# A head of bias moved from GpSimd and VectorE to TensorE in a log-sum-exp kernel, and larger loads

## The chip, the cores and the metric

The kernel runs on one core of one Trainium2 chip. The metric is the device time of one execution in microseconds; the runs shown are summed up by their median.

## The reference

Every row of `x` (8 batches, 2048 rows, 2048 columns, float32) is cut into 8 heads of 256 columns. A bias row of 256 is added to each head, and the log of the sum of exponentials is taken over each head's 256 columns; every result stands twice in a row, since the heads are repeated along the rows.

```python
x_heads = x.reshape(B, S, H, Dh).transpose(0, 2, 1, 3)
x_heads = x_heads + bias[None, :, None, :]
x_tiled = np.repeat(x_heads, 2, axis=2)
mx = x_tiled.max(axis=-1, keepdims=True)
lse = mx.squeeze(-1) + np.log(np.exp(x_tiled - mx).sum(axis=-1))
```

## The kernel before

A tile is 128 partitions x 2 rows x 2048 columns, 2 MB; there are 64, 8 for each batch. Eight tile buffers lie in SBUF as four blocks `xb` of 4 MB. The exponential is taken without the maximum (a check at the end, `judge`, repeats all with it if any sum is out of range).

Each tile of the long stage, 0 to 53 (`BULK`), is shared out by heads:

- Heads 0 to 2: TensorE puts the bias into PSUM (`put_bias`, L370: `ones_bf` against `b3`, the bias as three bfloat16 rows; for tiles 0 and 1, before `b3` is there, three one-row matmuls from `bparts` instead) and adds x with an identity matmul (`late_heads`, L428, float32, two passes each). Head 0 is in the bank `one_ps`, heads 1 and 2 in one of two `pair` tiles. ScalarE takes head 0's exponential with its sum (L439, one for each of the 2 rows) and writes the exponentials of heads 1 and 2 back to the tile (L446).
- Head 3: ScalarE takes its exponential without the bias, in place, and VectorE multiplies by exp(bias), which lies in PSUM as `w_ps` (L496).
- Heads 4 to 7: GpSimd adds the bias in place (`g_add`, L478, `b_rep`), ScalarE takes the exponential (L484, one instruction with head 3).
- VectorE sums heads 1 to 7 in one reduction (L503).

The order of the instructions on each engine is the order in which the code writes them (`tc.manual_schedule`). For tile t it is: x matmuls of t, GpSimd's add of t, then `later` of tile t-1 (L484, L496, L503) with the issue of a load (`reload`), then ScalarE's part of t, then the bias matmuls of t+1. Loads are issued by SyncE (SP); tiles 2 to 41 come as 4 MB blocks (L228), issued once both tiles of the block's buffer are done, tiles 0, 1 and 42 to 56 as 2 MB (L243), later ones in smaller pieces. `BLOCKS` is that limit.

Tiles 54 to 56 (`MIXED`) have heads 0 and 1 on TensorE, heads 2 and 3 weighed by VectorE (`weigh`, L519) and heads 4 to 7 on GpSimd; tiles 57 to 60 go by single rows, and the tail, 61 to 63, has an order written by hand (`TAIL`). They need exp(bias) of other heads in PSUM: `first_factors` makes heads 1 and 2 in `one_ps` after tile 53 (spread by TensorE at L303, exponential at L335), `other_factors` the rest at tile 32.

At the start the bias row comes in one 8 KB transfer (`brow`, L280), GpSimd splits it into the three bfloat16 parts (L293 to L297), and TensorE spreads heads 4 to 7 over the partitions (`spread`, L303), from which VectorE copies `b_rep` (L309).

Of the kernel before, what the change touches and what calls it, by code (L numbers as in the profile page):

```python
# [9 lines left out]
F32 = mybir.dt.float32  # L10
BF16 = mybir.dt.bfloat16
I32 = mybir.dt.int32
ACT = mybir.ActivationFunctionType
# [3 lines left out]

K = 2
KB = 4
BLOCKS = 42  # L20

NBUF = 8

NEARLY = 2

WARM = 384

# [17 lines left out]
STAGES = [  # L45
    (0, (BULK,)),
    (54, (MIXED,)),
# [45 lines left out]
def kernel(  # L93
# [6 lines left out]
    nc = tc.nc  # L100
    P = nc.NUM_PARTITIONS
    B, S, D = x.shape
    H, Dh = bias.shape
# [18 lines left out]

    brow = sb.tile([1, D], F32, name="brow")
    b_rep = sb.tile([P, D - G0], F32, name="b_rep")
# [91 lines left out]

    loads = {}
# [3 lines left out]
    def load(t):  # L221
        if TB <= t < BLOCKS:

# [32 lines left out]
    def reload(t):  # L256

        n = t + NBUF
        if n < BLOCKS:
            if n % TB == TB - 1:  # L260
# [41 lines left out]
    def spread(dst, c0, c1):  # L302
        nc.tensor.matmul(  # L303
            dst, lhsT=ones, rhs=brow[:, c0:c1], start=True, stop=True
        )

    for i, c in enumerate(range(G0, D, MM)):
        spread(ps[i], c, c + MM)
        nc.vector.tensor_copy(b_rep[:, c - G0 : c - G0 + MM], ps[i])  # L309
    W_LATE = BULK["g0"] * Dh  # L310
    w_late = w_ps[:, 0 : W_LATE - W0]
    spread(w_late, W0, W_LATE)
    nc.scalar.activation(out=w_late, in_=w_late, func=ACT.Exp)

    nc.vector.memset(Rx[0][:, 0:1], 4.0)
    nc.vector.memset(Rx[0][:, 1 + widths[0] :], 4.0)
# [1 line left out]
        out=b_far,  # L318
        in_=brow,
# [5 lines left out]
        out=Rx[0][0:1, 1 + widths[0] :],  # L325
# [6 lines left out]

    def first_factors():
        spread(one_ps, V0, W0)
        nc.scalar.activation(out=one_ps, in_=one_ps, func=ACT.Exp)  # L335

    def other_factors():
        nc.scalar.activation(
            out=w_ps[:, W_LATE - W0 :], in_=b_rep[:, W_LATE - G0 : W2 - G0], func=ACT.Exp
        )  # L340
        nc.scalar.activation(out=w_sb, in_=b_rep[:, W1 - G0 :], func=ACT.Exp)

# [13 lines left out]
    def put_bias(m, k0, k1):  # L356

        if m["late"]:  # L360
            pair = pairs[n_ps[0] % 2]
            n_ps[0] += 1
            got = [one_ps, pair[:, 0:MM], pair[:, MM : 2 * MM]]

            parts = [(ones_bf, b3)]
            if n_ps[0] <= NEARLY:
                parts = [(ones_bf[0:1], bparts[:, i]) for i in range(3)]
            for h, p in enumerate(got):
                for i, (lhsT, b) in enumerate(parts):
                    nc.tensor.matmul(  # L370
                        p,
                        lhsT=lhsT,
                        rhs=each_row(b, h * Dh, Dh, K),
                        start=i == 0,
                        stop=False,
                    )
            return got + [pair]
        n = m["pe"] * Dh
        rows = min(k1 - k0, max(MM // n, 1))
        got = []  # L380
        for k in range(k0, k1, rows):
            for c in range(0, n, MM):
                w = min(n - c, MM)
                bank = n_ps[0] % len(ps)
                p = ps[bank][:, 0 : rows * w]
                n_ps[0] += 1
                mm = nc.tensor.matmul(
                    p,
                    lhsT=ones_bf,
                    rhs=each_row(b3, c, w, rows),  # L390
                    start=True,
                    stop=False,
                )
                on_bank(bank, mm)
                got.append((k, k + rows, c, w, bank, p))
        return got
# [26 lines left out]
    def late_heads(m, t, got, sums):  # L423


        mms = []
        for h, p in enumerate(got[:-1]):
            mm = nc.tensor.matmul(  # L428
                p,
                lhsT=ident,  # L430
                rhs=xts[t % NBUF][:, :, h * Dh : (h + 1) * Dh],
                start=False,
                stop=True,
            )
            mms.append(on_x(t, mm, [loads[t, 0, 0]]))

        def pe_part():
            for k in range(K):
                act = nc.scalar.activation(  # L439
                    out=xts[t % NBUF][:, k, 0:Dh],  # L440
                    in_=got[0][:, k * Dh : (k + 1) * Dh],
                    func=ACT.Exp,
                    accum_out=sums[:, k, 0:1],
                )
                last_uses[t].append(on_x(t, act, [mms[0]]))
            act = nc.scalar.activation(  # L446
                out=xts[t % NBUF][:, :, Dh : m["pe"] * Dh].rearrange(
                    "p k (h j) -> p h k j", j=Dh
                ),
                in_=got[-1].rearrange("p (h k j) -> p h k j", k=K, j=Dh),  # L450
                func=ACT.Exp,
            )
            on_x(t, act, [mms[-1]])

        return pe_part

# [10 lines left out]
    def each_row(src, c, n, k_rows):  # L467

        return bass.AP(
            tensor=src.tensor,  # L470
            offset=src.offset + c,
            ap=[src.ap[0], [0, k_rows], [1, n]],
        )

    def g_add(m, t, k0, k1):
        c = m["g0"] * Dh
        v = xts[t % NBUF][:, k0:k1, c:D]
        add = nc.gpsimd.tensor_tensor(  # L478
            out=v, in0=v, in1=each_row(b_rep, c - G0, D - c, k1 - k0), op=ALU.add
        )  # L480
        return on_x(t, add, [loads[t, k0, 0]])
# [3 lines left out]

    def later(m, t, k0, k1, sums, add):

        h0 = m["pe"] if m["late"] else m["g0"]
        v = xts[t % NBUF][:, k0:k1, h0 * Dh : D]
        done = exp_inplace(t, v, add)  # L490
        if m["late"]:
            n = (m["g0"] - h0) * Dh
            f = v[:, :, 0:n]
            h0 = m["acc"]
            v = xts[t % NBUF][:, k0:k1, h0 * Dh : D]
            mul = nc.vector.tensor_tensor(  # L496
                out=f,
                in0=f,
                in1=each_row(w_ps, m["pe"] * Dh - W0, n, k1 - k0),
                op=ALU.mult,  # L500
            )
            done = on_x(t, mul, [done])
        red = nc.vector.tensor_reduce(  # L503
            out=sums[:, k0:k1, h0:H],
            in_=v.rearrange("p k (h j) -> p k h j", j=Dh),
            op=ALU.add,
            axis=mybir.AxisListType.X,
        )
        last_uses[t].append(on_x(t, red, [done]))

    def weigh(t, v, h, dst, after):
        c = h * Dh
        if c < W0:
            w = one_ps[:, c - V0 : c - V0 + Dh]
        elif c < W2:
            w = w_ps[:, c - W0 : c - W0 + Dh]
        else:
            w = w_sb[:, c - W1 : c - W1 + Dh]
        ttr = nc.vector.tensor_tensor_reduce(  # L519
            out=v,  # L520
            in0=v,
            in1=w,
            scale=1.0,
            scalar=0.0,
            op0=ALU.mult,
            op1=ALU.add,
            accum_out=dst,
        )
        last_uses[t].append(on_x(t, ttr, [after]))
# [329 lines left out]
    for t in range(T_TAIL):  # L859
        if t == T_FACTORS:  # L860
            other_factors()
        xt = xts[t % NBUF]
        sums = sums_of(t)
        for k0, k1, c0, c1 in pieces(t):
            m = modes_of(t)[k0]
# [28 lines left out]
            h0 = m["pe"]  # L894
# [107 lines left out]
```

## Time and profile before

| | us |
|---|---|
| median of 3 runs (322.25 to 322.52) | 322.31 |
| profiled execution, its own time | 322.15 |
| its span | 320.3 |
| TensorE busy (matmuls) | 247.0 |
| VectorE busy | 286.3 |
| ScalarE busy | 264.1 |
| GpSimd busy | 287.4 |

The span is the stretch that the profile covers; the rest of the execution's time lies around it. Busy time is the sum over instructions that compute; matmuls overlap one another, so TensorE's is not its throughput. The core read 134.23 MB and wrote 1.05 MB. In the profile PE is TensorE (PEld its weight loads), DVE VectorE, ACT ScalarE, POOL GpSimd, SP SyncE; L478 is line 478 of the kernel before.

### The profile page before, as it was taken

Reading aid. Unit: us, or ns where it says so; the run is one execution under the profiler, and the core shown is the slowest. Engines: PE = TensorE matmul, PEld = TensorE weight load, DVE = VectorE, ACT = ScalarE, POOL = GpSimd, SP = SyncE. Lnnn points to the kernel's source line nnn. Section 1 sums busy time; section 2 is a strip of 40 time slices with the busy share of each in tenths; the row PEclk is TensorE's granted clock in tenths of the full one; section 3 lists DMA queues with packets and bytes.
Section 4 is the critical chain, followed back from the end, with each engine's and each line's share of the span. In section 5 each row is a group of like instructions: output and inputs, shape, how many; then the busy total and the mean of one; then the engine's idle time right before and its main releaser. Section 6 shows DMA issues by size and latency. Waiting matters only on the chain.

```text
span 320.3 us, 2291 instructions
## 1 busy us (share of the span) xinstructions
PE 247.0 (77%) x621; PEld 100.5 (31%) x622; DVE 286.3 (89%) x304; ACT 264.1 (82%) x437; POOL 287.4 (90%) x116
## 2 busy tenths in 40 slices
PE   5998884877886677868688776988777787688774
PEld 1333332323332223323233322443333332133332
DVE  1337999699989999998989999799999999999996
ACT  1159987798788888779879988699889898999996
POOL 7939997999999999999999989999999999986874
PEclk9979996899799999979979998799999999799999
DMA  7999999999999999999999999999999999999996
GB/s 302 440 438 458 397 455 436 413 454 405 450 450 401 455 411 438 454 409 443 446 410 450 413 440 450 403 430 428 434 436 432 425 430 429 425 429 427 424 415 229
DMA packets 8950, 135.44 MB, mean 423 GB/s; under 512 B 996, under 2 KB 1511, under 8 KB 2791
## 3 DMA queue, kind: packets, MB, share of 16 engines
q1 hardware_dynamic: 8784, 135.14, 98.7%
q10 hardware_dynamic: 152, 0.14, 0.1%
q8 instruction: 5, 0.08, 0.1%
q14 instruction: 9, 0.07, 0.1%
HBM read 134.23 MB, written 1.05 MB: 422 GB/s over the span
## 4 chain that ended last, share of the span: by engine, by line
DMA 42%; POOL 18%; ACT 18%; DVE 13%; PE 8%; issue 0%; SPq 0%
DMA xb<-in_x_dram 41%; POOL xb L478 18%; ACT xb L484 12%; DVE R L503 11%; ACT xb L459 4%; PE pair L428 3%; DVE xb L496 2%; PE one_ps L428 2%; PE pair L303 1%; PE pair L370 1%; ACT xb L446 1%; DMA brow<-in_bias_dram 1%; PE one_ps L370 1%; ACT xb L439 1%; PE w_ps L303 0%
## 5 line engine op out<-in xcount | busy, mean ns | idle before, releaser
L478 POOL TENSOR_TENSOR xb<-xb,b_rep 128x2048 f32<-128x2048 f32 x57 | 257.6, 4545 | 18.9 <-DMA xb<-in_x_dram 18.9
L503 DVE TENSOR_REDUCE R<-xb 128x14 f32<-128x3584 f32 (+1 forms) x57 | 216.8, 3804 | 1.9
L484 ACT ACTIVATE xb<-xb 128x2560 f32<-128x2560 f32 (+8 forms) x79 | 156.8, 1996 | 18.2 <-POOL xb L478 18.2
L428 PE MATMUL pair<-xb,ident 128*128 128x512 f32 x216 | 110.0, 635 | 0.0
L428 PE MATMUL one_ps<-xb,ident 128*128 128x512 f32 x108 | 62.4, 661 | 17.1 <-DMA xb<-in_x_dram 17.1
L446 ACT ACTIVATE xb<-pair 128x1024 f32<-128x1024 f32 x54 | 55.5, 1029 | 18.2 <-PE pair L428 18.2
L428 PEld LDWEIGHTS pair<-xb,ident 128*128 128x128 f32 x216 | 44.5, 206 | 58.2 <-issue 58.2
L496 DVE TENSOR_TENSOR xb<-xb,w_ps 128x512 f32<-128x512 f32 x54 | 36.7, 679 | 22.3 <-ACT xb L484 22.3
L370 PE MATMUL one_ps<-b,ones_bf 128*128 128x512 bf16 x52 | 19.9, 382 | 38.0 <-ACT xb L439 38.0
L439 ACT ACTIVATE xb<-one_ps 128x256 f32<-128x256 f32 x108 | 40.0, 378 | 7.1 <-PE one_ps L428 7.0
L370 PEld LDWEIGHTS <-ones_bf 128*128 128x128 bf16 (+1 forms) x174 | 17.5, 101 | 85.5 <-issue 78.4
L370 PE MATMUL pair<-b,ones_bf 128*128 128x512 bf16 x104 | 31.1, 381 | 0.0
L428 PEld LDWEIGHTS one_ps<-xb,ident 128*128 128x128 f32 x108 | 19.8, 200 | 31.8 <-DMA xb<-in_x_dram 25.5
L439 ACT ACTIVATION_READ_ACCUMULATOR xb<-one_ps 128x1 f32 x108 | 22.1, 204 | 0.0
L519 DVE CUSTOM_DVE_ANT_0 xb<-xb,w_ps 128x256 f32<-128x256 f32 x60 | 22.0, 415 | 0.0
L405 PE MATMUL pair<-xb,ident 128*128 128x512 f32 x28 | 16.3, 685 | 5.5 <-DMA xb<-in_x_dram 5.3
L542 POOL TENSOR_TENSOR xb<-xb 128x128 f32<-128x128 f32 (+3 forms) x36 | 14.1, 392 | 3.3 <-ACT xb L832 0.5
L459 ACT ACTIVATE xb<-pair 128x256 f32<-128x256 f32 x39 | 15.2, 412 | 0.0
L536 POOL TENSOR_TENSOR xb<-xb,w_sb 128x256 f32<-128x256 f32 (+1 forms) x11 | 9.1, 827 | 4.4 <-ACT xb L484 3.9
L821 PE MATMUL pair<-xb,ident 128*128 128x256 f32 (+1 forms) x22 | 8.0, 456 | 3.2 <-DMA xb<-in_x_dram 3.2
L419 PE MATMUL tp<-b_rep,ident 128*128 128x384 f32 x24 | 9.7, 485 | 0.0
L459 ACT ACTIVATION_READ_ACCUMULATOR xb<-pair 128x1 f32 x39 | 9.3, 240 | 0.0
(61 smaller groups left out, 81.5 us busy)
## 6 DMA issues: line engine op xcount, KB each, us to landing
xb<-in_x_dram SPq DMA_DIRECT2D x20, 4096.0 KB, 22.0
xb<-in_x_dram SPq DMA_DIRECT2D x17, 2048.0 KB, 21.4
xb<-in_x_dram SPq DMA_DIRECT2D x10, 1024.0 KB, 21.7
xb<-in_x_dram SPq DMA_DIRECT2D x2, 640.0 KB, 18.2
xb<-in_x_dram SPq DMA_DIRECT2D x3, 384.0 KB, 12.3
xb<-in_x_dram SPq DMA_DIRECT2D x1, 768.0 KB
xb<-in_x_dram SPq DMA_DIRECT2D x2, 256.0 KB, 15.5
out_dram<-res SPq DMA_DIRECT2D x1, 512.0 KB, 5.8
```

What stands on the lines that cost most here:

```text
L370: nc.tensor.matmul(p, lhsT=lhsT, rhs=each_row(b, h * Dh, Dh, K), start=i == 0, stop=False,)
L405: mm = nc.tensor.matmul(p, lhsT=ident, rhs=xts[t % NBUF][:, ka:kb, c : c + w], start=False, stop=True,)
L428: mm = nc.tensor.matmul(p, lhsT=ident, rhs=xts[t % NBUF][:, :, h * Dh : (h + 1) * Dh], start=False, stop=True,)
L439: act = nc.scalar.activation(out=xts[t % NBUF][:, k, 0:Dh], in_=got[0][:, k * Dh : (k + 1) * Dh], func=ACT.Exp, accum_out=sums[:, k, 0:1],)
L446: act = nc.scalar.activation(out=xts[t % NBUF][:, :, Dh : m["pe"] * Dh].rearrange("p k (h j) -> p h k j", j=Dh), in_=got[-1].rearrange("p ...
L459: act = nc.scalar.activation(out=xts[t % NBUF][:, k, h * Dh : (h + 1) * Dh], in_=p, func=ACT.Exp, accum_out=sums[:, k, h : h + 1],)
L478: add = nc.gpsimd.tensor_tensor(out=v, in0=v, in1=each_row(b_rep, c - G0, D - c, k1 - k0), op=ALU.add)
L484: return on_x(t, nc.scalar.activation(out=v, in_=v, func=ACT.Exp), [after])
L496: mul = nc.vector.tensor_tensor(out=f, in0=f, in1=each_row(w_ps, m["pe"] * Dh - W0, n, k1 - k0), op=ALU.mult,)
L503: red = nc.vector.tensor_reduce(out=sums[:, k0:k1, h0:H], in_=v.rearrange("p k (h j) -> p k h j", j=Dh), op=ALU.add, axis=mybir.AxisListTy ...
L519: ttr = nc.vector.tensor_tensor_reduce(out=v, in0=v, in1=w, scale=1.0, scalar=0.0, op0=ALU.mult, op1=ALU.add, accum_out=dst,)
L542: done = nc.gpsimd.tensor_tensor(out=v[:, :, 0:n], in0=v[:, :, 0:n], in1=v[:, :, n : 2 * n], op=ALU.add)
```

## The change

- Head 3 of the long stage goes to TensorE too: a fourth bias matmul and a fourth x matmul for each tile, into a bank of its own, `wa_ps`, and an exponential of its own on ScalarE. The bias goes into the banks in the order of heads 1, 2, 0, 3, and x in the order 0, 3, 1, 2. ScalarE's exponential in place shrinks from 5 to 4 heads.
- VectorE multiplies 128 columns of head 4 (`N_LATE`) by exp(bias) instead of the 256 of head 3, and GpSimd adds the bias to heads 4 to 7 without these 128 columns.
- PSUM: `w_ps` is split into the banks `wa_ps` and `wb_ps`. `wa_ps` is in use until tile 53, so the factors of heads 3 and 4 are made by a second spread and exponential in `first_factors`; those of head 5's first 128 columns by `last_factors` before tile 56.
- The bias row comes in two transfers of four heads each; `CPE`, the columns that GpSimd splits into bfloat16 parts and the width of `b3`, grows from 768 to 1024. The spread of head 3 at the start is dropped.
- `BLOCKS` is 48 instead of 42: tiles 42 to 47 come as 4 MB blocks.

```diff
-BLOCKS = 42
+BLOCKS = 48
...
+LATE_BIAS = (1, 2, 0, 3)
+LATE_X = (0, 3, 1, 2)
...
-BULK = dict(pe=3, acc=1, g0=4, late=True, fold=0)
+BULK = dict(pe=4, acc=1, g0=4, late=True, fold=0)
+N_LATE = 128
...
-    w_ps = pp.tile([P, W2 - W0], F32, name="w_ps")
+    wa_ps = pp.tile([P, MM], F32, name="wa_ps")
+    wb_ps = pp.tile([P, MM], F32, name="wb_ps")
+    WB = W0 + MM
...
-    nc.scalar.dma_start(
-        out=brow.rearrange("p (h j) -> p h j", h=H), in_=bias.unsqueeze(0)
-    )
+    for h in range(0, H, H // 2):
+        nc.scalar.dma_start(
+            out=brow.rearrange("p (h j) -> p h j", h=H)[:, h : h + H // 2],
+            in_=bias[h : h + H // 2].unsqueeze(0),
+        )
...
-    W_LATE = BULK["g0"] * Dh
-    w_late = w_ps[:, 0 : W_LATE - W0]
-    spread(w_late, W0, W_LATE)
-    nc.scalar.activation(out=w_late, in_=w_late, func=ACT.Exp)
+    w_late = wb_ps[:, 0:N_LATE]
+    nc.scalar.activation(out=w_late, in_=b_rep[:, 0:N_LATE], func=ACT.Exp)
...
     def first_factors():
         spread(one_ps, V0, W0)
+        spread(wa_ps, W0, WB)
         nc.scalar.activation(out=one_ps, in_=one_ps, func=ACT.Exp)
+        nc.scalar.activation(out=wa_ps, in_=wa_ps, func=ACT.Exp)
+
+    def last_factors():
+        nc.scalar.activation(
+            out=w_late, in_=b_rep[:, WB - G0 : WB - G0 + N_LATE], func=ACT.Exp
+        )
...
-            got = [one_ps, pair[:, 0:MM], pair[:, MM : 2 * MM]]
+            got = [one_ps, pair[:, 0:MM], pair[:, MM : 2 * MM], wa_ps]
...
-            for h, p in enumerate(got):
+            for h in LATE_BIAS:
+                p = got[h]
...
             act = nc.scalar.activation(
-                out=xts[t % NBUF][:, :, Dh : m["pe"] * Dh].rearrange(
+                out=xts[t % NBUF][:, :, 3 * Dh : 4 * Dh],
+                in_=got[3].rearrange("p (k j) -> p k j", j=Dh),
+                func=ACT.Exp,
+            )
+            on_x(t, act, [mms[3]])
+            act = nc.scalar.activation(
+                out=xts[t % NBUF][:, :, Dh : 3 * Dh].rearrange(
                     "p k (h j) -> p h k j", j=Dh
                 ),
...
-        c = m["g0"] * Dh
+        c = m["g0"] * Dh + (N_LATE if m["late"] else 0)
...
-                in1=each_row(w_ps, m["pe"] * Dh - W0, n, k1 - k0),
+                in1=each_row(wb_ps, 0, N_LATE, k1 - k0),
...
+        if t == T_ROWS - 1:
+            last_factors()
```

More of the change, by code (lines that the diff above doesn't have):

```diff
@@ L334, in first_factors @@
         spread(one_ps, V0, W0)
+        spread(wa_ps, W0, WB)
         nc.scalar.activation(out=one_ps, in_=one_ps, func=ACT.Exp)
+        nc.scalar.activation(out=wa_ps, in_=wa_ps, func=ACT.Exp)
[3 more added lines that the diff above has]
+        )
     def other_factors():
         nc.scalar.activation(
-            out=w_ps[:, W_LATE - W0 :], in_=b_rep[:, W_LATE - G0 : W2 - G0], func=ACT.Exp
+            out=wb_ps[:, N_LATE:], in_=b_rep[:, WB - G0 + N_LATE : W2 - G0], func=ACT.Exp
         )
@@ L423, in late_heads @@
     def late_heads(m, t, got, sums):
-        mms = []
-        for h, p in enumerate(got[:-1]):
+        mms = {}
+        for h in LATE_X:
             mm = nc.tensor.matmul(
-                p,
+                got[h],
                 lhsT=ident,
@@ L434, in late_heads @@
             )
-            mms.append(on_x(t, mm, [loads[t, 0, 0]]))
+            mms[h] = on_x(t, mm, [loads[t, 0, 0]])
         def pe_part():
@@ L452, in pe_part @@
             )
-            on_x(t, act, [mms[-1]])
+            on_x(t, act, [mms[2]])
         return pe_part
@@ L486, in later @@
     def later(m, t, k0, k1, sums, add):
-        h0 = m["pe"] if m["late"] else m["g0"]
+        h0 = m["g0"]
         v = xts[t % NBUF][:, k0:k1, h0 * Dh : D]
@@ L491, in later @@
         if m["late"]:
-            n = (m["g0"] - h0) * Dh
-            f = v[:, :, 0:n]
+            f = v[:, :, 0:N_LATE]
             h0 = m["acc"]
@@ L514, in weigh @@
             w = one_ps[:, c - V0 : c - V0 + Dh]
+        elif c < WB:
+            w = wa_ps[:, c - W0 : c - W0 + Dh]
         elif c < W2:
-            w = w_ps[:, c - W0 : c - W0 + Dh]
+            w = wb_ps[:, c - WB : c - WB + Dh]
         else:
```

## The prediction

> **What bounds the kernel now.** I read the windows by stage first, then the starts of GpSimd's adds (the first work on a landed tile), then the chain that ended last. In the windows the columns after the stretch are the busy time of TensorE, its weight loads, VectorE, ScalarE and GpSimd, then TensorE's granted clock, the share of the 16 DMA engines and GB/s.
>
> ```profile
> 44.00:200.00 156.00, 117.31 (x291) 47.47 (x290) 146.12 (x67) 129.84 (x195) 144.41 (x33) 0.94 1.00 431
> 200.00:278.00 78.00, 62.28 (x160) 25.90 (x160) 75.57 (x37) 69.44 (x110) 77.05 (x18) 0.96 1.00 430
> 278.00:300.00 22.00, 18.14 (x46) 6.79 (x44) 22.00 (x84) 21.84 (x48) 17.38 (x25) 0.96 1.01 427
> 300.00:316.00 16.00, 12.32 (x47) 5.96 (x46) 15.97 (x95) 16.00 (x45) 12.68 (x24) 1.00 1.02 412
> ```
>
> The DMA share is 1.00 or more from 44 to 316 us, at 430 GB/s: the transfers never pause. No engine is busy for the whole of the long stage (VectorE 146.1 of 156 us, GpSimd 144.4), so a faster engine there only waits longer. From 278 us another limit appears: ScalarE is busy for 21.84 of 22 and 16.00 of 16 us.
>
> ```profile
> 42.07 9.05 POOL L478 TENSOR_TENSOR xb<-xb,b_rep 128x2048 f32<-128x2048 f32 x2 [0.61 <-DMA xb<-in_x_dram]
> 53.04 9.01 POOL L478 TENSOR_TENSOR xb<-xb,b_rep 128x2048 f32<-128x2048 f32 x2 [1.93 <-DMA xb<-in_x_dram]
> 62.71 9.04 POOL L478 TENSOR_TENSOR xb<-xb,b_rep 128x2048 f32<-128x2048 f32 x2 [0.66 <-DMA xb<-in_x_dram]
> ...
> 101.36 9.06 POOL L478 TENSOR_TENSOR xb<-xb,b_rep 128x2048 f32<-128x2048 f32 x2 [0.62 <-DMA xb<-in_x_dram]
> ...
> 208.05 67.67 POOL L478 TENSOR_TENSOR xb<-xb,b_rep 128x2048 f32<-128x2048 f32 x15 [0.62 <-DMA xb<-in_x_dram]
> 276.03 4.55 POOL L478 TENSOR_TENSOR xb<-xb,b_rep 128x2048 f32<-128x2048 f32 x1 [0.31 <-DMA xb<-in_x_dram]
> ```
>
> Each row is one run of adds, its third column onwards the operation and, in brackets, the wait before it. Two tiles land together in a 4 MB block. From 62.71 to 101.36 four blocks take 38.65 us, 9.66 a block or 4.83 a tile. From 208.05 (tiles 40 and 41 there) to 276.03 (tile 55) fourteen 2 MB tiles take 67.98 us, 4.856 each. One block, 42.07 to 53.04, took 10.97, 1.31 us over the rule.
>
> ```profile
> 276.03 4.56 POOL xb L478
> ...
> 280.61 2.86 ACT xb L484 x2
> ...
> 316.15 0.73 ACT xb L459 x4
> ```
>
> Read from the bottom, the end is ScalarE's last exponentials, 316.15, and everything on ScalarE back to 280.61, where it was released by GpSimd's add of tile 55 (276.03), which began when that tile landed. So the end is tile 55's landing, plus an add of 4.56 us, plus 36.3 us of ScalarE without a gap (to 316.88), plus 3.4 us to the span's end at 320.3. The change moves the time only through (a) when tile 55 lands and (b) whether ScalarE is free when its add is done. What reduces work of VectorE or GpSimd in the long stage is worth nothing by itself.
>
> **The change, part by part.** First the steady stage, tiles 0 to 53.
>
> ```profile
> L478 POOL TENSOR_TENSOR xb<-xb,b_rep 128x2048 f32<-128x2048 f32 x57 | 257.6, 4545 | 18.9 <-DMA xb<-in_x_dram 18.9
> L503 DVE TENSOR_REDUCE R<-xb 128x14 f32<-128x3584 f32 x54 | 210.0, 3888 | 1.9
> L484 ACT ACTIVATE xb<-xb 128x2560 f32<-128x2560 f32 x54 | 126.3, 2338 | 18.0 <-POOL xb L478 18.0
> ...
> L496 DVE TENSOR_TENSOR xb<-xb,w_ps 128x512 f32<-128x512 f32 x54 | 36.7, 679 | 22.3 <-ACT xb L484 22.3
> ...
> L484 ACT ACTIVATE xb<-xb 128x2048 f32<-128x2048 f32 x3 | 5.8, 1921 | 0.2 <-POOL xb L478 0.2
> ...
> L519 DVE CUSTOM_DVE_ANT_0 xb<-xb,one_ps 128x256 f32<-128x256 f32 x19 | 7.7, 412 | 0.0
> ```
>
> GpSimd: 1792 instead of 2048 elements a row, 4545 x 7/8 = 3977 ns, 0.57 us less a tile. VectorE: its product shrinks from 512 to 256 elements; the nearest row with 256 is 0.41 us, so 0.27 less, 4.30 a tile with the reduction. ScalarE: the exponential in place goes from 2560 to 2048 elements, 2338 to 1921 ns, 0.42 less; a new exponential of head 3 out of PSUM (512 elements) comes, 0.58 us by the row of L335 below. By the windows' first row ScalarE is busy for 129.84 of 156 us, 4.02 of each 4.83; it gets 4.2. All three stay under 4.83, so landings hide them.
>
> TensorE is the one that comes near. Starts of weight loads at 25.83 and 26.26 (rows of the start, below) show a step of 0.43 us for each of the two passes of a 512-column float32 matmul at full clock; at half clock it is 0.85 (15.34 and 16.19). A tile now needs 8 passes and 4 bfloat16 bias matmuls of half a step: 8 x 0.43 + 4 x 0.21 = 4.3 us, after 3.2. Under 4.83 at full clock; 8.5 at half.
>
> ```profile
> 17.10:20.50 3.40, 3.40 (x13) 1.25 (x12) 0.00 (x0) 2.92 (x2) 0.83 (x1) 0.96 1.00 434
> 20.50:23.90 3.40, 3.40 (x6) 1.17 (x5) 3.00 (x2) 1.17 (x5) 1.16 (x1) 0.53 1.07 463
> 136.60:140.00 3.40, 0.81 (x3) 0.19 (x2) 2.82 (x3) 2.88 (x7) 2.97 (x1) 0.96 1.07 463
> 140.00:143.40 3.40, 3.25 (x4) 1.50 (x5) 3.37 (x3) 2.78 (x5) 3.22 (x1) 0.54 1.05 453
> ```
>
> A stretch of 3.4 us with TensorE busy for only 0.81 (136.60) is followed by one at clock 0.54; so is the stretch from 17.10, which is busy throughout, but with nine bias matmuls of one row. The new kernel leaves TensorE 0.5 us idle a tile, so stretches like the first become rarer. I take full clock in the steady stage. The Trainium skill (TensorE: Matmul & The Clock Gate, Part 1) says that the clock halves after at least one idle window of about 3.4 us; the rows differ, for neither stretch was idle. By that rule nothing after the start would run at half clock and the first rival below would lose most of its chance; the sum would stay.
>
> Would slower steps starve the DMA queue? Not in the steady stage: loads are issued when VectorE has reduced a block's second tile, and by the rows of the start (first column the start, second the time) the first reload is issued 10 us before the queue is empty. There that margin is spent:
>
> ```profile
> 0.75 0.88 SPq L243 DMA_DIRECT2D xb<-in_x_dram  x2
> ...
> 3.02 0.82 POOL L293 CAST bparts<-brow 1x768 bf16<-1x768 f32 x1 [1.35 <-DMA brow<-in_bias_dram]
> ...
> 8.97 8.96 POOL L478 TENSOR_TENSOR xb<-xb,b_rep 128x2048 f32<-128x2048 f32 x2
> ...
> 9.93 2.76 PE L370 MATMUL pair<-bparts,ones_bf 1*128 1x512 bf16 x6
> ...
> 15.34 0.34 PEld L428 LDWEIGHTS pair<-xb,ident 128*128 128x128 f32 x1 [0.52 <-issue]
> ...
> 16.19 0.34 PEld L428 LDWEIGHTS pair<-xb,ident 128*128 128x128 f32 x1 [0.52 <-issue]
> ...
> 22.74 9.04 POOL L478 TENSOR_TENSOR xb<-xb,b_rep 128x2048 f32<-128x2048 f32 x2 [4.81 <-DMA xb<-in_x_dram]
> ...
> 25.83 0.19 PEld L428 LDWEIGHTS pair<-xb,ident 128*128 128x128 f32 x1 [0.24 <-issue]
> 26.26 0.19 PEld L428 LDWEIGHTS pair<-xb,ident 128*128 128x128 f32 x1 [0.24 <-issue]
> ...
> 28.10 3.89 DVE L503 TENSOR_REDUCE R<-xb 128x14 f32<-128x3584 f32 x1
> ```
>
> ```profile
> 32.06 0.33 SPq L228 DMA_DIRECT2D xb<-in_x_dram  x1
> ```
>
> GpSimd's split of the bias into three bfloat16 parts works on 1024 instead of 768 elements, a third more: the chain that lasted from 3.02 to the first add at 8.97 ends near 10.9. Tiles 0 and 1 each take 12 one-row bias matmuls, not 9, at 0.43 each while the clock is half (2.76 for six at 9.93), so the bias of tile 0 ends near 15.2 (the first needs the end of that chain). Its x matmuls are 8 passes, 6 at 0.85 and 2 at 0.43: 21. Tile 1's bias at 0.21: 23.5. Tile 1's x, half of it at half clock as the row from 20.50 shows: 29. Then the pair and the exponential in place on ScalarE (1.0 + 1.9), the product and the reduction on VectorE (0.4 + 3.89): 36.4, where the row at 28.10 ends at 31.99. So the first reload, at 32.06 before, goes out 4.4 us late. The queue lasts to 42.07. The first four tiles took 2.7 us more from the first issue to the add at 22.74 than their transfer (22.74 - 0.75 - 4 x 4.83), so a reload up to 39.4 costs nothing. Cover left: 3 us. The later reloads gain back 0.5 us a tile (4.30 against 4.83). The bias in two transfers, the dropped spread of head 3 and the exponential of 128 columns all lie under this cover: zero.
>
> Term 1, blocks: tiles 42 to 47 arrive at 4.83 instead of 4.856 us each, 6 x 0.025 = **-0.15 us** on the landing of tile 55. Their loads wait for two tiles' buffers instead of one, 4.5 us later, which the 10 us of queue hides. Bounds 0 and -0.3.
>
> Term 2, ScalarE's entry into the tail.
>
> ```profile
> 269.65 1.02 ACT L446 ACTIVATE xb<-pair 128x1024 f32<-128x1024 f32 x1
> 270.97 0.58 ACT L335 ACTIVATE one_ps<-one_ps 128x512 f32<-128x512 f32 x1 [0.29 <-PE one_ps L303]
> 271.46 3.27 ACT L484 ACTIVATE xb<-xb 128x2560 f32<-128x2560 f32 x2
> ...
> 280.61 1.91 ACT L484 ACTIVATE xb<-xb 128x2048 f32<-128x2048 f32 x1 [0.16 <-POOL xb L478]
> ```
>
> From 270.97 on ScalarE waits once, 0.16 us at 280.61. Into that stretch the change puts a second factor exponential at tile 53 (0.58, plus 0.15 of wait for its spread, which TensorE does after the first one) and one of 128 columns right before 280.61 (0.25, below the 0.41 of 256), and takes 0.42 from tile 53's exponential in place. 0.58 + 0.15 + 0.25 - 0.42 = 0.56; the gap of 0.16 absorbs some, and the new place of head 3's exponential lies earlier, in waits: **+0.35 us**. Before 270.97 nothing carries over, since tile 52's add is no longer late (GpSimd was behind without a break from 208.05 to 275.7). Bounds: 0, if the head start reaches through; +1.0, if the spreads cost two waits.
>
> Term 3, instruction loads.
>
> ```profile
> PE 247.0 (77%) x621; PEld 100.5 (31%) x622; DVE 286.3 (89%) x304; ACT 264.1 (82%) x437; POOL 287.4 (90%) x116
> ...
> q8 instruction: 5, 0.08, 0.1%
> ```
>
> The longer block at 42.07 shows that something may hold up a landing. The DMA engines also load instructions, five times 16 KB on q8. TensorE has 1243 instructions now and about 340 more after (four for each x matmul and two for each bias matmul make 6 a tile, 54 x 6, and the start's), so one or two loads more. The Trainium skill (DMA: Bandwidth & Descriptors, Queues, rings and completion order) says that each DMA engine takes turns between its queues packet by packet, so such a load would delay one engine's part of a block. No row shows which. Bounds from rows: 0 and +1.31; since the eleven blocks from 101.36 to 208.05 lose 0.4 us in all (106.69 against 11 x 9.66), I take **+0.15**.
>
> Sum: -0.15 + 0.35 + 0.15 = +0.35 us. On the profiled execution's 322.15 us (span 320.3 and 1.85 around it) that is 322.5; it lies 0.16 under the median 322.31, so the forecast median is 322.65.
>
> **The rivals.** A change of under 0.2%, 0.64 us, is about what a measurement of this kernel cannot tell from none.
>
> First, slower through the tail's entry: TensorE runs tile 53's matmuls at half clock. For it: clock 0.54 after thin stretches, and one-row spreads do not keep the clock. Against: tile 53 would have to follow a thin stretch, and TensorE is now busy 4.3 of 4.86 us. Price: four passes lose 0.42 us each, 1.7 us before the pair of tile 53, and every later step of ScalarE moves by it: 322.65 + 1.5 = 324.2. It decides where TensorE is busy for less than about a quarter of the 3.4 us before 266 us. 14%.
>
> Second, slower through the start: if all matmuls to tile 1 ran at half clock, x(0) ends at 22, bias(1) at 27, x(1) at 34, and the reload goes at 41.2 instead of 36.4, 1.8 us after the point of 39.4: 324.4. 8%.
>
> Third, the engines' head start absorbs term 2 and no landing is held up: -0.15, 322.2. 7%.
>
> Fourth, faster: the 1.31 us that the block after 42.07 lost does not occur in the changed kernel, whose loads are issued at other moments: 322.65 - 1.3 = 321.35. Against it: TensorE's code grows. 9%.
>
> **How the numbers follow.** The forecast case has 62%, from 322.2 to 323.2; about a seventh of it lies above +0.64. Faster by over 0.2%: the fourth, 0.09. Slower: 0.09 of the forecast case, 0.13 of the first rival, 0.08 of the second, 0.30. Within: 0.53 + 0.01 + 0.07 = 0.61. The range leaves out the fourth and the upper half of the two slow cases: 322.0 to 324.0.
>
> **What would show it.** Right, if the DMA share is 1.00 from 44 to 316 us again; the first reload is issued at 35 to 39 us; GpSimd's adds take 3.98 us and wait for DMA at every block; tiles 42 to 47 land in 9.66 us a block; ScalarE takes tile 55's exponential in place at 280.6 to 281.3 and has no gap after. Wrong, if the DMA share has a hole near 42 us, if TensorE's clock is lower than 0.94 in the steady stage and GpSimd waits longer than a landing explains, or if ScalarE has gaps after 281.

## The result, and the profile after

| | median us | runs | against before |
|---|---|---|---|
| before, beside it | 322.44 | 6 (322.25 to 322.85) | |
| after | 325.19 | 6 (324.59 to 326.42) | ratio 1.0089 [1.0066, 1.0111] |

The change makes the kernel 2.75 us slower, outside the forecast range of 322.0 to 324.0. The profiled execution of the kernel after took 325.20 us, its span 323.4.

The windows by stage first, with the columns as before (busy time of TensorE, weight loads, VectorE, ScalarE and GpSimd; TensorE's granted clock; DMA share; GB/s).

```profile
44.00:200.00 156.00, 147.64 (x409) 63.83 (x409) 146.33 (x70) 140.51 (x241) 126.45 (x33) 1.00 1.01 432
200.00:278.00 78.00, 75.53 (x209) 32.94 (x209) 70.14 (x37) 68.83 (x119) 68.63 (x18) 1.00 1.00 429
```

Transfers are as dense as before, TensorE's clock is 1.00, VectorE and GpSimd have more room than before. TensorE is busy for 75.53 of 78 us from 200 us on. Two lines of the page: the busy times of the engines, and the instruction loads, six now.

```profile
PE 290.3 (90%) x787; PEld 124.9 (39%) x788; DVE 274.4 (85%) x304; ACT 269.9 (83%) x493; POOL 260.1 (80%) x116
...
q8 instruction: 6, 0.10, 0.1%
```

Now the starts of GpSimd's adds; where an add waits for DMA, its start is a landing.

```profile
42.29 7.96 POOL L498 TENSOR_TENSOR xb<-xb,b_rep 128x1792 f32<-128x1792 f32 x2 [1.68 <-DMA xb<-in_x_dram]
53.56 7.98 POOL L498 TENSOR_TENSOR xb<-xb,b_rep 128x1792 f32<-128x1792 f32 x2 [3.32 <-DMA xb<-in_x_dram]
...
228.27 7.96 POOL L498 TENSOR_TENSOR xb<-xb,b_rep 128x1792 f32<-128x1792 f32 x2 [1.70 <-DMA xb<-in_x_dram]
237.93 23.79 POOL L498 TENSOR_TENSOR xb<-xb,b_rep 128x1792 f32<-128x1792 f32 x6 [1.70 <-DMA xb<-in_x_dram]
...
267.14 4.01 POOL L498 TENSOR_TENSOR xb<-xb,b_rep 128x1792 f32<-128x1792 f32 x1 [0.83 <-DMA xb<-in_x_dram]
...
276.82 4.55 POOL L498 TENSOR_TENSOR xb<-xb,b_rep 128x2048 f32<-128x2048 f32 x1 [0.31 <-DMA xb<-in_x_dram]
```

From 228.27 to 237.93 a block lands in 9.66 us, up to the pair of tiles 46 and 47 at 237.93. Tile 53 lands at 267.14 and tile 55 at 276.82, 0.79 later than before (276.03); the block after 42.29 took 11.27 us. That is under a third of the loss. The rest is in the chain that ended last (start, duration, instruction), from the last pair on:

```profile
238.40 0.86 PE one_ps L442 x2
...
242.69 0.86 PE one_ps L442 x2
...
255.58 0.44 PE tp L589 x4
...
269.10 0.86 PE one_ps L442 x2
...
272.53 1.05 PE one_ps L311 x2
273.58 0.87 PE wa_ps L311 x2
274.48 0.58 ACT wa_ps L343
...
283.48 0.17 ACT wb_ps L346
283.65 2.77 ACT xb L504 x2
```

Before, this chain reached tile 55 through GpSimd's add. Now it is TensorE from the last pair to the factors (`spread`, L311), then ScalarE without a pause to 319.81. TensorE starts x of tile 46 at 238.40 and x of tile 47 at 242.69, 4.76 us after both landed. Tile 53 it starts at 269.10, 1.96 us after its landing. So in six tiles it won back 2.80 us, 0.47 a tile: its starts lie 26.41 us apart (4.40 a tile, in which the transposes at 255.58 took 0.44 once) and the landings 29.21 (4.87 a tile). The rest of the delay goes into ScalarE's queue. It takes tile 55's exponential in place at 283.65, 6.8 us after the landing, where before it was 4.58 (280.61 after 276.03). So 0.8 us of landing and 2.2 us of queue make 3.0 us, and ScalarE's end moved by 2.9 (316.88 to 319.81).

### The profile page after: what moved, and what is told of

Its sections match the earlier page's. It is cut to its first block, busy times and chain, and to the rows that moved or that the text cites. A ratio compares the mean times of both kernels' runs of the same rounds, so it can differ in the third digit from the quotient of the medians.

```text
span 323.4 us, 2676 instructions
## 1 busy us (share of the span) xinstructions
PE 290.3 (90%) x787; PEld 124.9 (39%) x788; DVE 274.4 (85%) x304; ACT 269.9 (83%) x493; POOL 260.1 (80%) x116
## 4 chain that ended last, share of the span: by engine, by line
DMA 30%; DVE 25%; PE 25%; ACT 18%; issue 1%; SPq 0%
DMA xb<-in_x_dram 28%; DVE R L522 23%; ACT xb L504 11%; PE pair L442 8%; PE one_ps L442 5%; PE wa_ps L442 4%; ACT xb L479 4%; PE pair L384 2%; DVE xb L515 2%; DMA brow<-in_bias_dram 2%; PE pair L311 1%; ACT xb L466 1%; PE wa_ps L384 1%; PE one_ps L384 1%; PE tp L433 0%
## 5 line engine op out<-in xcount | busy, mean ns | idle before, releaser
L498 POOL TENSOR_TENSOR xb<-xb,b_rep 128x1792 f32<-128x1792 f32 (+1 forms) x57 | 228.5, 4030 | 47.6 <-DMA xb<-in_x_dram 45.0
L504 ACT ACTIVATE xb<-xb 128x2048 f32<-128x2048 f32 (+7 forms) x79 | 134.0, 1711 | 0.0
L442 PE MATMUL pair<-xb,ident 128*128 128x512 f32 x216 | 102.5, 597 | 0.0
L442 PE MATMUL one_ps<-xb,ident 128*128 128x512 f32 x108 | 58.7, 626 | 10.8 <-DMA xb<-in_x_dram 10.8
L442 PE MATMUL wa_ps<-xb,ident 128*128 128x512 f32 x108 | 56.7, 608 | 0.0
L515 DVE TENSOR_TENSOR xb<-xb,wb_ps 128x256 f32<-128x256 f32 x54 | 22.7, 420 | 31.6 <-ACT xb L504 31.4
L384 PEld LDWEIGHTS <-ones_bf 128*128 128x128 bf16 (+1 forms) x232 | 22.9, 100 | 48.9 <-issue 32.9
L460 ACT ACTIVATE xb<-wa_ps 128x512 f32<-128x512 f32 x54 | 32.5, 602 | 1.8 <-PE wa_ps L442 1.5
L442 PEld LDWEIGHTS wa_ps<-xb,ident 128*128 128x128 f32 x108 | 21.1, 195 | 26.9 <-issue 26.9
L384 PE MATMUL wa_ps<-b,ones_bf 128*128 128x512 bf16 x52 | 19.7, 379 | 0.0
L419 PE MATMUL pair<-xb,ident 128*128 128x512 f32 x28 | 16.3, 687 | 2.0 <-DMA xb<-in_x_dram 2.0
```

The costliest lines, as they stand in the source:

```text
L384: nc.tensor.matmul(p, lhsT=lhsT, rhs=each_row(b, h * Dh, Dh, K), start=i == 0, stop=False,)
L419: mm = nc.tensor.matmul(p, lhsT=ident, rhs=xts[t % NBUF][:, ka:kb, c : c + w], start=False, stop=True,)
L442: mm = nc.tensor.matmul(got[h], lhsT=ident, rhs=xts[t % NBUF][:, :, h * Dh : (h + 1) * Dh], start=False, stop=True,)
L460: act = nc.scalar.activation(out=xts[t % NBUF][:, :, 3 * Dh : 4 * Dh], in_=got[3].rearrange("p (k j) -> p k j", j=Dh), func=ACT.Exp,)
L498: add = nc.gpsimd.tensor_tensor(out=v, in0=v, in1=each_row(b_rep, c - G0, D - c, k1 - k0), op=ALU.add)
L504: return on_x(t, nc.scalar.activation(out=v, in_=v, func=ACT.Exp), [after])
```

## The experiments

Theory at this point: the 4 MB blocks up to tile 47 cost the time. The second tile of a pair is a whole tile's work late on the slowest engine, and too few tiles of 2 MB follow to make that up before the tail, which has no gap for it. The expectations of the first runs call this theory 1; the rivals there are ScalarE's added exponentials at the hand-over and the late start. The experiments were timed in five rounds, each beside the kernel before; microseconds over it are (ratio - 1) x 322.4. Line numbers shift by a few lines between kernels; the operations tell which is which.

| kernel | blocks up to tile | bias transfers | ratio to before | us over it |
|---|---|---|---|---|
| after | 47 | 2 | 1.0089 [1.0066, 1.0111] | 2.9 |
| after, no `keep_warm` at the last block | 47 | 2 | 1.0070 [1.0057, 1.0084] | 2.3 |
| after, one bias transfer | 47 | 1 | 1.0073 [1.0060, 1.0086] | 2.4 |
| after, blocks to 43 | 43 | 2 | 1.0022 [1.0010, 1.0034] | 0.7 |
| after, blocks to 41 | 41 | 2 | 1.0032 [1.0018, 1.0046] | 1.0 |
| after, blocks to 41, one bias transfer | 41 | 1 | 1.0015 [1.0006, 1.0024] | 0.5 |
| the same, factors made ready | 41 | 1 | 1.0010 [1.0001, 1.0019] | 0.3 |
| the same, tiles 54 and 55 shared out anew | 41 | 1 | 1.0014 [1.0005, 1.0023] | 0.5 |
| the same, TensorE kept busy | 41 | 1 | 1.0008 [0.9999, 1.0017] | 0.3 |
| before, blocks to 47 | 47 | 1 | 1.0049 [1.0036, 1.0062] | 1.6 |
| before, blocks to 45 | 45 | 1 | 1.0025 [1.0016, 1.0034] | 0.8 |
| before, two bias transfers | 41 | 2 | 1.0016 [1.0007, 1.0025] | 0.5 |

**Blocks to tile 41 in the kernel after.**

```diff
-BLOCKS = 48
+BLOCKS = 42
```

> The changed kernel with 4 MB blocks only to tile 41 again. Theory 1 (TensorE's backlog: it needs 4.30 us a tile against 4.84 of a landing, gains only 0.54 a tile after a pair that lands together, and so is 1.8 us behind at tile 53 when the last pair is 46/47): the last pair is 40/41, the backlog of 4.4 us is gone by tile 50, ScalarE takes tile 55's exponential 0 to 0.4 us after its add instead of 2.1, and the time is 1.75 us less, 323.4. Theory 2 (the two extra factor exponentials and their spread on ScalarE alone make it late): no change, 325.2 and 0.15 more for the smaller loads. Theory 3 (the start: second half of the bias at 6.9 us, first reload at 39.67 into a queue about to be empty): no change, 325.2 to 325.4.

Measured 323.18 us (322.93 to 325.31), against 323.4 by theory 1 and 325.2 or more by its rivals; the ratio's interval lies clear below that of the kernel after. The profiled execution is the slowest of the seven, with late landings (325.31 us), so its rows are read against its own landings. First tile 55's landing and its exponential, then TensorE's waits between 228.3 and 274.5 us:

```profile
278.46 4.54 POOL L498 TENSOR_TENSOR xb<-xb,b_rep 128x2048 f32<-128x2048 f32 x1 [0.31 <-DMA xb<-in_x_dram]
...
283.37 1.96 ACT L504 ACTIVATE xb<-xb 128x2048 f32<-128x2048 f32 x1
```

```profile
PE one_ps L442 <- DMA xb<-in_x_dram: 0.8, 3, 0.3
```

The exponential starts 4.91 us after the landing, not 6.8. TensorE waits for loads again at each of the last three tiles: it is not behind when the tail begins.

**Blocks to tile 43.** A backlog that is made up has a threshold; a price for each block has none.

```diff
-BLOCKS = 48
+BLOCKS = 44
```

> The changed kernel with 4 MB blocks to tile 43 in place of 47. If the cost is the last pair's second tile, a tile's time late on TensorE, of which each later tile wins back 0.54 us, then ten tiles stand between tile 43 and the hand-over, enough for the whole: the time is that of blocks to 41, 323.2 us on the scale of the kernel before at 322.4 us (0.8 us over it), and TensorE waits for loads again before tile 53. If each block costs the same, the 2.0 us over three blocks, it is 0.67 us more: 323.9 us (1.5 us over).

Measured 322.80 us against 322.31, a ratio that leaves 0.3 to 1.1 us: the flat case; 1.5 us is outside. TensorE's x of tile 53 and GpSimd's add of it (its landing):

```profile
267.38 1.12 PE L442 MATMUL one_ps<-xb,ident 128*128 128x512 f32 x2 [0.27 <-DMA xb<-in_x_dram]
267.41 4.00 POOL L498 TENSOR_TENSOR xb<-xb,b_rep 128x1792 f32<-128x1792 f32 x1 [0.84 <-DMA xb<-in_x_dram]
```

Tile 53 is the first after the last pair for which this view shows TensorE waiting, and for 0.27 us only: the ten tiles from 44 to 53, at about 0.47 each, are just enough for a delay like the 4.76 us of the kernel after.

**The same blocks in the kernel before, to 47 and to 45.** There TensorE has 1.6 us to spare in each tile, but GpSimd, at 4.51 (49.64 us for 11 adds below), wins back only 0.34 from a landing of 4.856.

```diff
-BLOCKS = 42
+BLOCKS = 48
```

> The kernel before with 4 MB blocks to tile 47. Theory 1: TensorE at 3.2 us a tile has lost the pair's lag two tiles later, GpSimd (4.55) and VectorE (4.57) gain 0.3 a tile and stay behind to tile 53; if ScalarE waits for them there the time rises by 1 us or more, if only TensorE's order counts it is 322.3, 0.15 less. Rival: the larger blocks cost by themselves, whatever TensorE has to do (buffers freed two at a time, queue shorter): 323.5 or more, with a gap in the transfers.

Measured 323.97 us (323.87 to 324.04). GpSimd's adds, then ScalarE's exponential of tile 55:

```profile
237.09 49.64 POOL L478 TENSOR_TENSOR xb<-xb,b_rep 128x2048 f32<-128x2048 f32 x11 [0.63 <-DMA xb<-in_x_dram]
```

```profile
282.25 2.90 ACT L484 ACTIVATE xb<-xb 128x2048 f32<-128x2048 f32 x2
```

No transfer is late: the pair lands at 237.09, blocks 9.66 us apart as before. The adds run for 49.64 us without a pause, so that the tenth, tile 55's, ends at about 282.2, and ScalarE takes it at 282.25 instead of 280.61, 1.64 later; the time is 1.6 us longer. The theory holds with another engine as the slow one.

```diff
-BLOCKS = 42
+BLOCKS = 46
```

> The kernel before with 4 MB blocks to tile 45. GpSimd's add (4.53 us) wins back 0.345 us for each tile that lands after the last pair; to tile 47 the cost was 1.6 us. With two tiles more to win back, 0.69 us less: tile 55's add ends 0.95 us later than in the kernel before, and the time is 0.9 us over it, 323.2 to 323.3 us, with GpSimd's adds without a pause to tile 54. Rival: the blocks cost by themselves, each the same: 1.07 us over, which this run can hardly tell apart; the trace can, by whether GpSimd has made up its delay when tile 55 lands.

Measured 323.12 us against 322.31. The same two views:

```profile
227.27 58.58 POOL L478 TENSOR_TENSOR xb<-xb,b_rep 128x2048 f32<-128x2048 f32 x13 [0.62 <-DMA xb<-in_x_dram]
```

```profile
281.42 2.91 ACT L484 ACTIVATE xb<-xb 128x2048 f32<-128x2048 f32 x2
```

Two tiles more, and the exponential starts at 281.42, 0.81 after the kernel before; the time is 0.8 us longer, as against the 0.9 expected. GpSimd is still behind when tile 56 has landed.

**One bias transfer.**

```diff
-    for h in range(0, H, H // 2):
-        nc.scalar.dma_start(
-            out=brow.rearrange("p (h j) -> p h j", h=H)[:, h : h + H // 2],
-            in_=bias[h : h + H // 2].unsqueeze(0),
-        )
+    nc.scalar.dma_start(
+        out=brow.rearrange("p (h j) -> p h j", h=H), in_=bias.unsqueeze(0)
+    )
```

> The changed kernel with the bias in one transfer again. TensorE's first spread goes back from 7.06 to about 3.1 us and the first reload from 39.67 to about 36. Theory 1: only the landings move, by the 0.3 to 0.5 us that the queue's gap near 42 us costs; the backlog at tile 53 stays 1.8 us: 324.7. Theory 3: most of the loss comes back, 323.0 or less. Theory 2: as theory 1 at most.

Measured 324.72 us, as theory 1 expected. The rival that the start explains most of the loss falls. What the second transfer does is seen in the kernel after: the first spread waits for it until 7.06 us, and the first reload is issued at 39.67.

```profile
7.06 2.04 PE L311 MATMUL pair<-brow,ones 1*128 1x512 f32 x2 [7.06 <-DMA brow<-in_bias_dram]
```

```profile
39.67 17.52 SPq L234 DMA_DIRECT2D xb<-in_x_dram  x3
```

With one transfer the first spread began at 2.91 us, and the first reload was issued at 34.02, not 36. Windows of one microsecond show no hole in the transfers after 42 us that the kernel before does not have: from 42 to 46 us the DMA share was 0.72, 0.84, 1.17 and 1.06 in the kernel after, and 1.21, 1.14, 0.30 and 0.99 before. The landings show more. Three profiles had their first reload at 39.5 us or later, and there the block that follows the landing at 42 us took 11.27 us (the kernel after), 13.09 (blocks to 41) and 11.61 (blocks to 43). In the ten others the reload went out between 30.49 and 38.01 us, and that block took 10.79 to 11.10 us. This fits the forecast's point of 39.4 us, but no run moves the reload alone.

**Two bias transfers in the kernel before.** The edit is the same, the other way round.

> The kernel before with the bias in two transfers, nothing else: the cost of the second transfer alone. If what it costs is the late first reload (its second half lands near 6.9 us, the first reload comes at 36 us or later, and the queue of loads runs thin at 42 us): 0.3 to 0.5 us, 322.7 to 322.9 us. Rival: the kernel before has GpSimd adding 128x2048 and keeps pace after all, the first reload stays ahead of 37 us and nothing is lost: 322.4 us.

Measured 322.79 us against 322.25: 0.5 us, as expected. Two other pairs of kernels differ by as much, 1.0089 against 1.0073 and 1.0032 against 1.0015, but within each of them the intervals overlap; this run alone is clear. Where the time is lost is not settled. The late reload, which the expectation blamed, is not enough: here it went out at 36.0 us and the block behind it took 11.00 us (10.97 before), and the next kernel's went out at 38.01 with only one transfer. ScalarE's last instruction, before and here:

```profile
317.29 0.38 ACT L737 ACTIVATE res_last<-pair 128x256 f32<-128x256 f32 x1 [0.42 <-PE pair L731]
```

```profile
317.46 0.38 ACT L739 ACTIVATE res_last<-pair 128x256 f32<-128x256 f32 x1 [0.42 <-PE pair L733]
```

It is 0.17 us later, while the span is 0.7 longer (321.0 against 320.3). The rest of that difference lies behind the issue of the last output, a stretch that lasts from 2.6 to 3.1 us in the thirteen profiles, so one profile cannot place half a microsecond.

**Blocks to 41 and one bias transfer together.**

```diff
-BLOCKS = 48
+BLOCKS = 42
...
+    nc.scalar.dma_start(
+        out=brow.rearrange("p (h j) -> p h j", h=H), in_=bias.unsqueeze(0)
+    )
```

> The changed kernel with 4 MB blocks to tile 41 and the bias in one transfer, so that only the heads' new shares, the order of the matmuls and the factors are left of the change. If the costs of the blocks (2.0 us) and of the second bias transfer (0.47 us) stand beside each other, 322.7 us, and the first reload is issued at 34 us. What is left over the kernel before, 0.3 us, is ScalarE's: tile 55's exponential in place starts about 4.9 us after its tile has landed, where it is 4.58 us before. Rival: the 0.47 us of the bias were part of the same backlog on TensorE and are not there with blocks to 41: 323.2 us.

Measured 322.78 us against 322.25. The two costs stand beside each other: 1.0089 less 0.0057 for the blocks less 0.0016 for the transfer is 1.0016, and 1.0015 was measured. Tile 55's add and its exponential, and the first reload:

```profile
276.16 4.54 POOL L496 TENSOR_TENSOR xb<-xb,b_rep 128x2048 f32<-128x2048 f32 x1 [0.35 <-DMA xb<-in_x_dram]
...
281.08 2.91 ACT L502 ACTIVATE xb<-xb 128x2048 f32<-128x2048 f32 x2
```

```profile
38.01 17.50 SPq L234 DMA_DIRECT2D xb<-in_x_dram  x3
```

ScalarE starts 4.92 us after the landing, 0.34 later than before, and without a wait. The reload was expected at 34 us; in the five kernels with one transfer and the heads' new shares it was issued anywhere from 34.00 to 38.01.

**Without `keep_warm` at the last block.** TensorE's two `keep_warm` steps lie between its x matmuls of tile 45 and those of tile 46, where every microsecond should count.

```diff
-                if t == BLOCKS - TB - 1:
-                    keep_warm()
...
-                    if t == BLOCKS - TB - 1:
-                        keep_warm()
```

> The changed kernel without the two matmuls that only keep TensorE's clock up at tile 45 (1.3 us of TensorE, between the last pair's bias and x). Theory 1: the backlog at tile 53 falls from 1.8 to 0.5 us and the time by 1.3, 323.9; the clock stays full, since TensorE is busy without a break there. Theory 2 and 3: 325.2; a rise if the clock halves.

Measured 324.57 us, 0.6 less than the kernel after and not 1.3, and the two intervals overlap. TensorE's x of tiles 46 and 53, and GpSimd's add of 53; then x of tile 53 in the same view of the kernel after:

```profile
237.23 1.12 PE L442 MATMUL one_ps<-xb,ident 128*128 128x512 f32 x2 [0.81 <-DMA xb<-in_x_dram]
...
268.03 1.02 PE L442 MATMUL one_ps<-xb,ident 128*128 128x512 f32 x2
```

```profile
266.32 4.01 POOL L498 TENSOR_TENSOR xb<-xb,b_rep 128x1792 f32<-128x1792 f32 x1 [0.86 <-DMA xb<-in_x_dram]
```

```profile
268.93 1.02 PE L442 MATMUL one_ps<-xb,ident 128*128 128x512 f32 x2
```

x of tile 46 starts on its landing (a wait of 0.81 for DMA), yet tile 53's starts 1.71 us after its own. In this view, whose starts lie 0.17 before those of the chain, the kernel after has 1.79 (268.93 after 267.14). So the backlog fell by 0.08 us, not by the 1.3 expected. In the kernel after the two steps ran for the most part before the pair had landed, so they had cost the backlog little; I had counted their whole time. Tile 55 landed 0.76 us sooner in this profile, which the edit does not explain.

**Factors made ready.** ScalarE's two exponentials at the hand-over are replaced by one on a single partition at tile 32, and TensorE spreads its result.

```diff
-        spread(one_ps, V0, W0)
-        spread(wa_ps, W0, WB)
-        nc.scalar.activation(out=one_ps, in_=one_ps, func=ACT.Exp)
-        nc.scalar.activation(out=wa_ps, in_=wa_ps, func=ACT.Exp)
+        for p, c in ((one_ps, 0), (wa_ps, MM)):
+            nc.tensor.matmul(
+                p, lhsT=ones, rhs=brest[:, 0, c : c + MM], start=True, stop=True
+            )
...
     def other_factors():
+        nc.scalar.activation(out=brest[:, 0], in_=brow[:, V0:WB], func=ACT.Exp)
```

> The kernel of the other run (blocks to 41, one bias transfer), and the factors of heads 1 to 4 and a half made ready: ScalarE takes their exponentials on one partition in the middle of the run (one instruction of 1x1024, about 1 us, in its slack), and TensorE spreads the exponentials at the hand-over; the two 128x512 exponentials (0.58 us each) and the wait of 0.28 us between them are gone from ScalarE's way there. If ScalarE's entry is what is left of the loss, tile 55's exponential in place starts at its add's end, 4.58 us after the landing, and the time is 322.4 us, that of the kernel before. Rival: the loss of 0.3 us comes from another place (the start, instruction loads): 322.7 us, with ScalarE waiting for GpSimd.

Measured 322.60 us. Add and exponential of tile 55:

```profile
276.26 4.54 POOL L497 TENSOR_TENSOR xb<-xb,b_rep 128x2048 f32<-128x2048 f32 x1 [0.30 <-DMA xb<-in_x_dram]
...
280.84 2.86 ACT L503 ACTIVATE xb<-xb 128x2048 f32<-128x2048 f32 x2 [0.36 <-POOL xb L497]
```

ScalarE now waits for GpSimd, 4.58 us after the landing, as in the kernel before. The exponential moved by 0.34 against the landing, and the time went from 1.0015 to 1.0010: between the expectation and its rival, and the intervals overlap. ScalarE's last instruction, with blocks to 41 and one transfer, and with the factors ready too:

```profile
317.78 0.38 ACT L756 ACTIVATE res_last<-pair 128x256 f32<-128x256 f32 x1 [0.42 <-PE pair L750]
```

```profile
317.79 0.38 ACT L757 ACTIVATE res_last<-pair 128x256 f32<-128x256 f32 x1 [0.42 <-PE pair L751]
```

So ScalarE's earlier start brought nothing to its end. Its start at tile 55 is 0.24 us sooner (280.84 against 281.08), but behind 301 us it meets the tail's loads: TensorE waits for them until 301.27 and 306.14, and ScalarE's exponentials begin beside it, at 301.25 and 306.12. Without the edit the same loads are there at 301.26 and 306.13, and ScalarE comes to them at 301.42 and 306.17. In the kernel before they land 0.5 us sooner, at 300.76 and 305.62, while tile 55's landing is only 0.13 and 0.23 sooner there. What remains of the loss goes with these landings; why they are later is not shown.

**Tiles 54 and 55 shared out like those before them.**

```diff
+MIXED_N = dict(MIXED, n=128)
...
-    (54, (MIXED,)),
+    (54, (MIXED_N,)),
+    (56, (MIXED,)),
...
-        c = m["g0"] * Dh + (N_LATE if m["late"] else 0)
+        c = m["g0"] * Dh + (N_LATE if m["late"] else m.get("n", 0))
...
-        if m["late"]:
+        if m["late"] or "n" in m:
             f = v[:, :, 0:N_LATE]
-            h0 = m["acc"]
+            h0 = m["acc"] if m["late"] else h0
```

`last_factors` moves behind ScalarE's sums of tile 56.

> As the kernel with the factors made ready, and tiles 54 and 55 are shared out between GpSimd and VectorE as the tiles before them: GpSimd biases 128x1792 (3.98 us) where it was 128x2048 (4.53 us), VectorE multiplies 128x256 (0.42 us). If GpSimd's add of tile 55 is what ScalarE then waits for, its exponential in place starts 0.55 us sooner, 4.0 us after the landing, and the rest follows without a gap: 321.85 us. Rival 1: ScalarE's own work before it takes its place, it gains 0.2 us or less: 322.2 us. Rival 2: VectorE, with 0.42 us more for each of two tiles, comes late in the tail, or the tail waits for its last loads, and nothing is gained: 322.4 us.

Measured 322.84 us: no gain. All engines from tile 55's landing on, then two windows:

```profile
276.27 3.99 POOL L499 TENSOR_TENSOR xb<-xb,b_rep 128x1792 f32<-128x1792 f32 x1 [0.88 <-DMA xb<-in_x_dram]
...
280.29 2.86 ACT L505 ACTIVATE xb<-xb 128x2048 f32<-128x2048 f32 x2 [0.57 <-POOL xb L499]
...
281.13 3.57 PE L420 MATMUL pair<-xb,ident 128*128 128x512 f32 x4 [2.48 <-DMA xb<-in_x_dram]
...
284.74 0.38 ACT L480 ACTIVATE xb<-pair 128x256 f32<-128x256 f32 x1 [0.87 <-PE pair L420]
```

```profile
277.80:281.20 3.40, 0.93 (x4) 0.17 (x2) 3.37 (x8) 2.83 (x10) 2.50 (x2) 1.00 1.01 426
281.20:284.60 3.40, 3.40 (x5) 1.16 (x6) 3.37 (x11) 2.68 (x6) 3.40 (x1) 0.53 1.01 426
```

The exponential does start at 280.29, 4.02 us after the landing. But TensorE, idle for 2.48 us before tile 56, takes its four matmuls in 3.57 us at clock 0.53, and ScalarE stands for 0.87 us. Neither rival had named that.

**The same, with TensorE kept busy.**

```diff
+            if "n" in m:
+                for _ in range(1 + t - T_PROMPT):
+                    keep_warm()
```

> The kernel with the factors made ready and tiles 54 and 55 shared out as those before them, and TensorE kept busy there: one keep_warm after tile 54's matmuls and two after tile 55's, in its idle time. In the run without them tile 55's exponential did start 4.0 us after the landing, but tile 56's matmuls ran at a lower granted clock (3.57 us for four instead of 1.98 us) and ScalarE then waited 0.87 us for them. If that clock ate the gain, the four take 1.98 us, the wait is gone, tile 57's exponential starts at 284.5 to 284.7 us, and the time is 322.0 to 322.1 us, 0.2 us under the kernel before. Rival: the tail's loads hold the rest back, since they land when they landed before: ScalarE is 0.5 us early at 285 us, waits for loads later on, and the time is 322.4 to 322.6 us.

Measured 322.69 us against 322.31. The same views, and a later row of ScalarE:

```profile
276.38 4.00 POOL L499 TENSOR_TENSOR xb<-xb,b_rep 128x1792 f32<-128x1792 f32 x1 [0.88 <-DMA xb<-in_x_dram]
...
278.61 1.45 PE L434 MATMUL tp<-b_rep,ident 128*128 128x384 f32 x4
...
280.42 2.86 ACT L505 ACTIVATE xb<-xb 128x2048 f32<-128x2048 f32 x2 [0.57 <-POOL xb L499]
...
281.25 1.98 PE L420 MATMUL pair<-xb,ident 128*128 128x512 f32 x4 [1.19 <-DMA xb<-in_x_dram]
```

```profile
277.80:281.20 3.40, 2.26 (x8) 0.91 (x6) 3.37 (x10) 2.83 (x10) 2.58 (x1) 1.00 1.03 434
281.20:284.60 3.40, 3.12 (x7) 1.17 (x8) 3.37 (x11) 3.40 (x10) 3.33 (x1) 1.00 1.01 426
```

```profile
301.46 1.48 ACT L505 ACTIVATE xb<-xb 128x1536 f32<-128x1536 f32 x1 [0.22 <-DMA xb<-in_x_dram]
```

The clock is 1.00, tile 56's matmuls take 1.98 us and the wait is gone. Still nothing is gained against the kernel with the factors made ready: at 301.46 ScalarE waits for a load of the tail. So the rival holds, and the tail has two limits close together, ScalarE's queue and the landings. No version here beats the kernel before.

## Why the prediction was wrong

**Term 1 failed, in its sign.** It priced the blocks at -0.15 us, with bounds 0 and -0.3, because it looked only at when tiles land. The landings came as forecast, 9.66 us a block. But a pair lands for both its tiles at the time of the second, and the engines then take them one after the other: measured +1.8 us in the kernel after (0.0057 of the time with two bias transfers, 0.0058 with one) and +1.6 us in the kernel before. The row that tells it stood in the prediction: after 208.05 GpSimd ran 15 adds without a pause, those of the last pair, 40 and 41, and of all 13 tiles from there to 54. So the pair's delay took that long to make up. I read it as GpSimd being behind and asked of tile 52's add alone whether it "carries over". I had worked out TensorE's 4.3 us a tile, and did not multiply the half microsecond of slack by the six tiles that were left: 2.8 us of the 4.8 needed.

**Term 2 held** for the moment that it priced. +0.35 us for ScalarE's entry was forecast; with the blocks and the bias put back, tile 55's exponential starts 0.34 us later after its landing. Its worth in time is not shown. With the factors made ready the exponential is back at 4.58 us after the landing, but ScalarE's last instruction starts at 317.79 instead of 317.78, since the tail's loads hold it up. The prediction had put all of the tail down to ScalarE; the loads lie close behind.

**Term 3** forecast one or two instruction loads more; there was one. Its +0.15 us was not measured by itself. With one transfer tile 55 lands 0.13 and 0.23 us later than before (276.16 and 276.26 against 276.03) and the tail's loads 0.5 us later; no run tests whether an instruction load does that.

**The start** was forecast as free. The bias in two transfers was put under cover without asking when the second half lands, and it carries heads 4 to 7, which the first spread needs. So the reload came at 39.67 instead of 36.4, just behind the point of 39.4, and the block behind it took 11.27 us where it took 10.97 before. The transfer costs 0.5 us, and the late reload is not the whole of that.

**TensorE in the steady stage** was right: 4.30 us a tile, clock 1.00, adds of 3.98 us. Of the rivals the two slow ones (324.2 and 324.4 us) came nearest in time, but the clock was 1.00 at tile 53, and the reload went out at 39.67, not 41.2. None of the four was a backlog that lasts into the tail. Of the signs that the prediction named as right, two failed: the reload (39.67, not 35 to 39) and tile 55's exponential (283.65, not 280.6 to 281.3).

Sum of what was measured: blocks 1.8, second transfer 0.5, the rest 0.5 us. For the rest the traces show two limits side by side, ScalarE's entry and the tail's later loads; its cause stays open.

## What to carry to other kernels

Larger loads are priced at the end of the stage that uses them, too: after the last large one, (tiles left) x (landing interval - slowest engine's time a tile) must cover a whole tile's work, or the next stage starts late by the rest. An engine that gets more work in a stage where it still fits has less with which to catch up, so the point up to which large loads are free moves. A transfer that is split to start sooner is worth what its last needed half is worth.

## What was not expected of the hardware

TensorE's clock fell to 0.53 behind a window of 3.40 us in which it was busy for 0.93 us, with no idle stretch over 2.48 us; with 1.45 us of dummy matmuls in that gap it stayed at 1.00. The Trainium skill (TensorE: Matmul & The Clock Gate, Part 1) ties the lower clock to at least one idle window of about 3.4 us; these rows show it after a window that was only thin.

The second of two bias transfers of 4 KB, issued right behind the first, released its reader at 7.06 us, where one transfer of 8 KB released it at 2.91.
